# A two-layer decoder trunk on one core: joint 16 x 16 inverses for four heads, an SBUF region of its own for the first loads, and more of the modulation on VectorE

## The chip, the core and the metric

The kernel runs on one core of a Trainium2 chip. The metric is the device time of one execution in microseconds (us). "PE" is TensorE (its weight loads are listed apart as PEld), DVE is VectorE, ACT is ScalarE, POOL is GpSimd, SP is SyncE, which issues nearly all DMAs.

## The reference

The input x is [1, 256, 2048] and goes through two layers. In each layer six modulation rows m = 0 to 5 come from the condition c. They shift, scale and gate the two halves of a layer.

```python
c_act = jax.nn.silu(c)
for l in range(2):
    mod = c_act @ w_ada[l] + b_ada[l]              # [2048] x [2048, 6*2048]
    sh_m, sc_m, gt_m, sh_f, sc_f, gt_f = split(mod, 6)
    h = rms_norm(x, ln_mix[l]) * (1 + sc_m) + sh_m
    proj = h @ w_in[l]
    # 8 delta-net heads of 128 (q, k, v, gate z, beta, decay)
    # and 16 attention heads of 64 (2 kv heads, window 128, sinks, rope)
    mix = concat(gated_deltanet(...), attention(...)) @ w_out[l]
    x = x + gt_m * mix
    h = rms_norm(x, ln_ffn[l]) * (1 + sc_f) + sh_f
    gate, up = split(h @ w_gate_up[l], 2)          # 2 x 5632 columns
    x = x + gt_f * ((silu(gate) * up) @ w_down[l])
return rms_norm(x, ln_final)
```

A delta-net head works in chunks of 64 positions. Per chunk it needs the inverse of a unit lower triangular 64 x 64 matrix, then two products with it, then a recurrence over the four chunks:

```python
lower = where(strict, (k*beta) @ k.T * decay, 0) + eye
t_inv = triangular_solve(lower, eye)
w, u  = t_inv @ (k*beta*exp(g)), t_inv @ (v*beta)
```

## The kernel before

**Matrix products.** All weights are fp32 (603 MB are read). Each 128 x 1024 piece of weights is loaded by one DMA from the SP queue (line 115, called from `Weights.load`). A part of four 128 x 128 blocks is then split into a rounded copy `wh` (a cast on ACT) and a remainder `wl` (a subtraction on DVE, or on POOL when `Weights.split`, lines 336 to 365, finds GpSimd free outside the FFN). A block then costs three PE matmuls of 256 columns (tiles `pm`, in the head stages) or one of 512 and one of 256 (output projection and FFN). The activations sit in tiles `act`. All compute instructions pass through one helper, so that the profile gives them line 155; they are told apart by their tiles.

**Order.** Nothing is ordered by a scheduler at run time: the program counts a clock for each engine from prices (`Timed`, line 96) and emits each engine's instructions in the order in which this clock says they could go. Side work is written as generators in `Steps` (lines 217 to 285): each says which engine its next instructions go to, and is let forward 300 ns after its last one. Between two matmuls of a projection `S.tick()` lets them forward. `S.wait()` moves the clock by 100 ns where nothing can go. On the chip each engine then works strictly in that order.

**Stages.** (1) The first stage makes the modulations m = 1 and m = 0 of layer 0 and, while they become known k block by k block, partial projections of 28 tiles (`EARLY`, `GROUPS`). (2) The heads of layer 0. (3) The output projection of layer 0. (4) The FFN of layer 0. Then heads, output projection and FFN of layer 1. In the profile of before they lie at 0 to about 215, to 498, to 619, to 1381, to 1750, to 1845 and to 2604 us. These bounds are read from the first instruction that only the next stage has.

**Modulation** (`Ada`, line 457). A piece of w_ada is 128 x 1024 (tile `wada`, three buffers, 512 KB). Rows of layer 0 with m in `COLS` = (1, 0, 2, 4) are PE products (`products`, line 498): four matmuls 32 x 256 for each of 128 pieces, 8 records each in the trace. All others are DVE rows (`rows`, line 566): one multiply-and-sum instruction over 128 x 1024 for each piece (the profile calls it CUSTOM_DVE_ANT_0, the order below ISA), and after every second piece one 128 x 1 addition to `mod`. A table of due times says by which weight unit how many pieces must have been loaded. Before the first row, c's activation is spread over 128 partitions by four matmuls with `con` (line 534), after the last product.

**A delta-net head** (`delta`, line 1163). Scores k k^T and k q^T on PE; `B`, their product with decay and beta; `mc`, the sixteen 16 x 16 diagonal blocks gathered to 128 x 32 (lines 1227 to 1238). They are inverted for each head alone: `R` (line 1240), one fp32 matmul of 128 x 512 with it, then 30 chained multiply-and-sum instructions on DVE into `uc` (two for each of 15 columns, lines 1251 to 1259). `U` spreads `uc` to block diagonals (line 1264), PE transposes it together with v (`vT`, lines 1274 to 1277), and steps of 16, 32 and 64 rows make the whole inverse (tiles `W`, `y`, `yn`, lines 1289 to 1379). Then the recurrence, the norm and the gate follow.

Two heads may be in this part at once. `JOBS` (line 36) orders the projections: for each head k, q, an attention pair two ahead, v, z. Head h's v projection waits until head h - 2 has set "mid". This is set at line 1306, behind the copy of the first transposes and ahead of the steps of 16, 32 and 64.

## Time and profile before

| what | us |
|---|---|
| median of 3 runs | 2602.87 (2583.37 to 2609.12) |
| the profiled execution | 2606.06 |
| its span | 2604.2 |
| mean granted clock of TensorE | 0.983 |
| PE busy | 2500.6 (96%) |
| DVE busy | 1944.2 (75%) |
| ACT busy | 1281.5 (49%) |
| POOL busy | 417.9 (16%) |

The span is what the profiler shows from the first to the last instruction; 1.9 us of the execution lie around it. A share of busy time is an average over seven stages whose limits differ, so the table alone tells no stage's limit; the stretches in the prediction do.

### The profile page before, as it was taken

The numbers are of one execution on the slowest core, as the hardware profiler recorded it, in microseconds if no ns is written. First come the engines' busy times: TensorE is split into PE (matmuls) and PEld (weight loads), VectorE is DVE, ScalarE is ACT, GpSimd is POOL, SyncE is SP. The second block draws the span as 40 slices with busy tenths as digits, with TensorE's granted clock in tenths as the row PEclk, the third lists the DMA queues.
The fourth block names the chain that finished last, engine by engine and source line by source line (L and its number), as shares of the span: only waits on it lengthen the run. The fifth ranks groups of instructions, "written<-read, shape, count | busy, mean of one in ns | idle before, by whom it ended". The sixth has DMA issues, their size and how long they took to land.

```text
span 2604.2 us, 45895 instructions
## 1 busy us (share of the span) xinstructions
PE 2500.6 (96%) x16398; PEld 2148.0 (82%) x16398; DVE 1944.2 (75%) x4831; ACT 1281.5 (49%) x2759; POOL 417.9 (16%) x375
## 2 busy tenths in 40 slices
PE   6999999888999999999999899999899999999998
PEld 4777777777888888888888788998788888888887
DVE  3647777998777888888997877787877766555565
ACT  3225555335455444454445565644555544555553
POOL 2223333552000000000003443345000000000000
PEclk9999999999999999999999899999899999999999
DMA  8888664675777899999996433346577766555564
GB/s 279 294 286 290 241 211 171 222 253 187 259 253 252 311 323 323 324 328 330 324 346 204 163 123 121 130 162 203 194 265 249 261 187 188 196 190 188 184 195 137
DMA packets 184088, 608.62 MB, mean 234 GB/s; under 512 B 19121, under 2 KB 30513, under 8 KB 183857
## 3 DMA queue, kind: packets, MB, share of 16 engines
q1 hardware_dynamic: 183858, 605.68, 68.4%
q8 instruction: 128, 2.10, 0.3%
q14 instruction: 102, 0.84, 0.1%
HBM read 603.51 MB, written 2.10 MB: 233 GB/s over the span
## 4 chain that ended last, share of the span: by engine, by line
PE 42%; issue 30%; DVE 6%; ACT 1%; POOL 0%; POOLq 0%; DVEq 0%; ACTq 0%
PE pr L155 19%; PE psm L155 12%; PE pm L155 10%; DVE wl L155 1%; DVE wada L155 1%; DVE x L155 1%; ACT wh L155 0%; DVE act L155 0%; DVE R L155 0%; DVE mc L155 0%; DVE ry L155 0%; DVE sp_y L155 0%; DVE cv L155 0%; DVE do L155 0%; DVE B L155 0%
## 5 line engine op out<-in xcount | busy, mean ns | idle before, releaser
L155 ACT CAST wh<-w 128x512 fp32r<-128x512 f32 (+1 forms) x1566 | 900.9, 605 | 408.1 <-PE psm L155 137.7
L155 DVE TENSOR_TENSOR wl<-w,wh 128x512 fp32r<-128x512 f32 (+1 forms) x1317 | 893.3, 698 | 249.9 <-ACT wh L155 240.0
L155 PE MATMUL pr<-act,wh 128*128 128x512 f32 x2816 | 993.0, 397 | 10.8 <-DVE kq L155 7.5
L155 PE MATMUL pr<-act,wl 128*128 128x256 f32 x2816 | 792.8, 282 | 0.0
L155 PE MATMUL pm<-act,wh 128*128 128x256 f32 (+1 forms) x2816 | 658.6, 320 | 13.8 <-DVE x L155 5.0
L155 PEld LDWEIGHTS pr<-act,wh 128*128 128x128 f32 x2816 | 531.4, 189 | 137.5 <-DVE kq L155 8.1
L155 PE MATMUL psm<-act,wh 128*128 128x512 f32 (+1 forms) x1792 | 569.4, 373 | 1.8 <-ACT wh L155 0.9
L155 POOL TENSOR_TENSOR wl<-w,wh 128x512 fp32r<-128x512 f32 (+1 forms) x249 | 344.3, 1388 | 1272.0 <-ACT wh L155 1174.2
L155 PEld LDWEIGHTS pm<-act,wh 128*128 128x128 f32 x2816 | 462.7, 194 | 88.9 <-issue 44.6
L155 PEld LDWEIGHTS pr<-act,wl 128*128 128x128 f32 x2816 | 535.7, 190 | 0.0
L155 PE MATMUL pm<-act,wl 128*128 128x256 f32 x1664 | 474.3, 285 | 1.3 <-POOL wl L155 1.3
L155 PE MATMUL psm<-act,wl 128*128 128x256 f32 x1600 | 450.5, 282 | 1.7 <-POOL wl L155 1.7
L155 PEld LDWEIGHTS psm<-act,wh 128*128 128x128 f32 x1792 | 325.6, 190 | 72.5 <-issue 9.0
L155 DVE CUSTOM_DVE_ANT_0 wada<-wada,cs 128x1024 f32<-128x1024 f32 x256 | 325.5, 1274 | 36.6 <-DMA wada<-w_ada 36.2
L155 PEld LDWEIGHTS pm<-act,wl 128*128 128x128 f32 x1664 | 322.4, 194 | 2.2 <-POOL wl L155 1.7
L155 PEld LDWEIGHTS psm<-act,wl 128*128 128x128 f32 x1600 | 304.0, 190 | 2.7 <-POOL wl L155 2.1
L155 ACT COPY kq<-pr 128x512 f32<-128x512 f32 x88 | 51.8, 589 | 206.7 <-PE pr L155 206.6
L155 POOL TENSOR_TENSOR n2r<-ms,halfc 128x2 f32<-128x2 f32 x5 | 3.5, 691 | 797.9 <-DVE ms L155 797.9
L155 DVE TENSOR_TENSOR kq<-pr,kq 128x512 f32<-128x512 f32 x88 | 60.6, 688 | 92.8 <-ACT kq L155 92.8
L155 DVE SCALAR_TENSOR_TENSOR x<-psm,mod,x 128x256 f32<-128x256 f32 x128 | 61.9, 483 | 70.4 <-PE psm L155 67.9
L155 PE MATMUL psm<-wada,cs 128*32 128x256 f32 x1024 | 86.7, 414 | 17.7 <-DMA wada<-w_ada 17.5
L155 ACT CAST act<-kq 128x256 fp32r<-128x256 f32 x88 | 35.8, 407 | 74.0 <-DVE kq L155 74.0
(176 smaller groups left out, 1752.1 us busy)
## 6 DMA issues: line engine op xcount, KB each, us to landing
wada<-w_ada SPq DMA_DIRECT2D x384, 512.0 KB, 5.5
w<-w_gu SPq DMA_DIRECT2D x352, 512.0 KB, 4.6
w<-w_in SPq DMA_DIRECT2D x147, 512.0 KB, 4.0
w<-w_dn SPq DMA_DIRECT2D x128, 512.0 KB, 4.6
w<-w_out SPq DMA_DIRECT2D x64, 512.0 KB, 4.3
w<-w_dn SPq DMA_DIRECT2D x64, 384.0 KB, 4.2
w<-w_in SPq DMA_DIRECT2D x28, 384.0 KB, 4.9
x<-xT SPq DMA_DIRECT2D x4, 512.0 KB, 7.5
```

The lines of the kernel that those rows point to most:

```text
L155: return f(*a, **k)
```

## The change

**First stage.** `COLS` is (1,): only m = 1 of layer 0 is still made by PE products (32 pieces). Its 32 products alternate with the 32 pieces of m = 0, which are now DVE rows, and m = 2 and m = 4 (64 pieces) are DVE rows too. The first 64 pieces get eight buffers `wx` in a region laid out for this stage alone (before: three `wada`). Of the early weights every second piece gets one of four more buffers (`wy`) beside the four of `w`. c is spread (`spread`) at the start. Between the first stage and the heads stands a barrier: the head tiles are laid out when all of `hs`, the 64 first pieces and the first loads are done. FFN middles get eight tiles of their own (`mid`), and `act` goes from 38 to 30.

**Joint inverses.** `delta` is cut in three: `scores` per head up to `mc`, `inverses` per four heads, `delta` per head for the rest. `inverses` issues eight small DMAs on ACT's queue, which carry the `mc` of four heads to `qi` (64 partitions, one block in each, 256 elements). On DVE the block inverse is made in three doublings, 2 to 4 to 8 to 16, in `ui` (18 instructions, instead of four times 30). Eight DMAs bring it back to `uc`. R, its matmul and the subtraction ahead of it go. `JOBS` puts k and q of the next four heads ahead of the v of a batch. "mid" is now set behind the V transposes, which no longer stand with U's but behind the matmuls of the steps of 16, 32 and 64. The squares for q's norm move to `scores`; `y` exists twice (`y16`).

The order on the engines in the heads of layer 0, at the second batch (heads 4 to 7). On PE, before (`U` are the inverses of one head, `vT` its v, `con` the identity, `pm` a projection):

```order
L155 MATMUL pm_3078<-act_574,wh_2873 128x256 x2
L155 MATMUL pm_3078<-act_574,wl_2874 128x256
L155 MATMUL pm_3078<-act_630,wh_2873 128x256 x2
L155 MATMUL pm_3078<-act_630,wl_2874 128x256
L155 MATMUL psm_3103<-con_64,U_3047 128x128 x2
L155 MATMUL psm_3103<-con_64,vT_2557 128x128 x2
L155 MATMUL pm_3078<-act_955,wh_2916 128x256 x2
L155 MATMUL pm_3078<-act_955,wl_2917 128x256
L155 MATMUL psm_98<-wada_2985,cs_66 32x256 x4
```

and after, from the last projection matmuls ahead of the joint inverse (`w` and `av` are attention):

```order
L161 MATMUL pm_5176<-act_2091,wh_5105 128x256 x2
L161 MATMUL pm_5176<-act_2091,wl_5106 128x256
L161 MATMUL psm_5297<-con_67,w_1234_5090 128x128 x3
L161 MATMUL psm_5309<-w_1279_5291,av_2264 64x128
L161 MATMUL psm_5309<-w_1284_5307,av_2264 64x128
```

```order
L161 MATMUL psm_5415<-yn_5428,U_5372 32x32
L161 MATMUL psm_5445<-W_5381,B_3714 64x64 x2
L161 MATMUL psm_5451<-W_5383,B_3836 64x64 x2
L161 MATMUL psm_5445<-U_5369,yn_5412 64x64 x2
L161 MATMUL psm_5451<-U_5372,yn_5428 64x64 x2
L161 MATMUL psm_5460<-con_67,vT_4834 128x128 x2
L161 MATMUL pm_5465<-act_273,wh_5137 128x256 x2
L161 MATMUL pm_5465<-act_273,wl_5138 128x256
```

Before, the transposes of U and v stand between matmuls of a projection. After, the 41 rows from 1502 to 1543 hold no projection matmul; the stretch ends with the transposes of `vT`, behind which the v projection of head 6 begins. A stretch of that kind (65 rows, with 126 DVE instructions beside it) stands at the first batch of layer 0, and one of 41 rows at the second batch of layer 1. In before, none is longer than 16 rows.

On ACT, after, at the same batch (`x8` are eight DMA issues, `V` and `W` as above):

```order
L161 ACTIVATE w_1234_5090<-w_1234_5090,aden_5168 128x256
L161 DMA qi_5252<-mc_3727 8x16x16 x8
L161 CAST wh_5280<-w_5071 128x512
L161 COPY w_1279_5291<-psm_5274 128x384
L161 ACTIVATE th_5293<-pm_5176 128x256
L161 COPY w_1284_5307<-psm_5297 128x384
L161 CAST act_5321<-psm_5309 128x256
L161 ACTIVATE th_5323<-cv_5158 128x256
L161 DMA uc_5360<-ui_2104 128x1x16 x8
L161 COPY W_5381<-psm_5375 128x256
```

The two groups of DMA issues stand between casts, copies and the activations of attention. Whatever follows the second group on ACT waits with it for `ui`.

On DVE, before, at the inverse of one head, and after, at the joint one:

```order
L155 TENSOR_TENSOR mc_2840<-mc_2840,con_64 128x32
L155 TENSOR_TENSOR R_2843<-mc_2840,con_64 128x512
L155 TENSOR_TENSOR act_367<-pm_2743,act_367 128x256
L155 TENSOR_TENSOR wl_2874<-w_2642,wh_2873 128x512
L155 TENSOR_TENSOR act_2867<-psm_2848,act_2867 128x256
L155 TENSOR_TENSOR act_367<-pm_2822,act_367 128x256
```

```order
L161 ISA wada_5156,n_1282_5303<-wada_5156,cs_69 128x1024
L161 ISA n_1282_5303 128x1
L161 COPY ui_2104<-qi_5252 64x8
L161 SCALAR_TENSOR_TENSOR cv_5158<-pm_5057,par_66,cv_5158 128x253
L161 ISA wada_5278,n_1282_5303<-wada_5278,cs_69 128x1024
L161 ISA n_1282_5303 128x1
L161 COPY ui_2104<-qi_5252 64x4x2x2
L161 TENSOR_TENSOR hi_5325<-ui_2104 64x8
L161 TENSOR_TENSOR ui_2104<-ui_2104,hi_5325 64x4x2
```

Rows of the modulation (`wada`) now stand between the steps of the inverse. Counted over the whole order, the DVE rows (pieces) are 0, 10 and 23 in the first stage, the heads and the output projection of layer 0 before, and 36 (32 of them `wx`), 53 and 39 after; later stages keep theirs. Parts of weights split by POOL are 39, 57 and 39 in these stages before, 39, 50 and 29 after.

The diff, cut to its core:

```diff
-NACT = 38
+NACT, NMID = 30, 8
...
+AHEAD, BATCH = 2, 4
 JOBS = [("ak", 0), ("av", 0)] + [("aq", h) for h in range(AHEAD)]
+for _h in range(BATCH):
+    JOBS += [("k", _h), ("q", _h)] + [("aq", AHEAD + _h // 2)] * (_h % 2)
 for _h in range(H):
-    JOBS += [("k", _h), ("q", _h)] + [("aq", _h + AHEAD)] * (_h + AHEAD < H) + [("v", _h), ("z", _h)]
+    JOBS += [("v", _h), ("z", _h)]
+    for _n in range(BATCH, H):
+        if _n - BATCH == _h:
+            JOBS += [("k", _n), ("q", _n), ("aq", _n)]
...
-COLS = (1, 0, 2, 4)
-ROWS = [(0, m) for m in (2, 4, 3, 5) if m not in COLS] + [(1, m) for m in (1, 0, 2, 4, 3, 5)]
+COLS = (1,)
+ROWS = [(0, m) for m in (0, 2, 4, 3, 5)] + [(1, m) for m in (1, 0, 2, 4, 3, 5)]
...
+    def tag(self, u):
+        return "wy" if u < self.marks["mix0"] and u % 2 else "w"
+    def room(self):
+        u = self.loaded
+        return sum(self.tag(v) == self.tag(u) for v in self.tiles) < self.BUFS
...
-                self.todo = [(0, m, j, i) for j in range(8) for m in (1, 0) for i in range(4)]
-                self.todo += [(0, m, j, i) for m in COLS[2:] for j in range(8) for i in range(4)]
-                self.cols = len(self.todo)
-                self.todo += [(l, m, k, i) for l, m in ROWS for k in range(KT) for i in range(2)]
-                self.last = {it[:2]: n + 1 for n, it in enumerate(self.todo)}
+                self.todo = []
+                for j in range(8):
+                    for i in range(4):
+                        self.todo += [(True, 0, 1, j, i), (False, 0, 0, 2 * j + i // 2, i % 2)]
+                self.first = len(self.todo)
+                self.todo += [(False, l, m, k, i) for l, m in ROWS[1:] for k in range(KT) for i in range(2)]
+                self.last = {it[1:3]: n + 1 for n, it in enumerate(self.todo)}
+                self.order = [n for n, it in enumerate(self.todo) if not it[0]]
...
-                        (135, "out0"), (162, "ffn0"), (192, "down0"), (345, "mix1"), (345, "out1"), (352, "ffn1"), (384, "down1")
+                        (110, "out0"), (160, "ffn0"), (192, "down0"), (340, "mix1"), (345, "out1"), (352, "ffn1"), (384, "down1")
...
+            def room(self):
+                n = self.nload - self.ndone
+                return n < (b.total["wx"] if self.nload < self.first else self.BUFS)
...
-                while self.ready and self.nstart < self.nload and self.tiles[self.nstart][1] <= S.now():
-                    n = self.nstart
+                while self.ready and self.nstart < len(self.order):
+                    n = self.order[self.nstart]
+                    if n not in self.tiles or self.tiles[n][1] > S.now():
+                        return
                     if (hush and n >= self.force) or not b.free["n2"]:
                         return
                     behind = max(0, self.want(u) - n)
-                    slack = 100 + 150 * behind if n >= self.force else 2000
+                    slack = 3000 if n < self.first else 100 + 150 * behind if n >= self.force else 2000
...
-        def delta(l, h, st, outs):
+        def scores(l, h, st, bt):
...
+            if "mc" not in bt:
+                bt["mc"], bt["n"] = b.t("mc", [128, BATCH, 2, 16], bufs=1), 0
             nc.vector.tensor_reduce(
-                out=mc, in_=mo.rearrange("p a (m c) -> p a c m", c=16), op=ALU.add, axis=mybir.AxisListType.X
+                out=bt["mc"][:, h % BATCH, :, :], in_=mo.rearrange("p a (m c) -> p a c m", c=16), op=ALU.add,
+                axis=mybir.AxisListType.X,
             )
             b.give("do")
+            st.update(B=B, qn=qn, rk=rk)
+            bt["n"] += 1
+            if bt["n"] == BATCH:
+                S.add(inverses(bt, bt["ui"]), 0)
+        def inverses(bt, ui):
+            yield A_
+            qi = b.t("qi", [64, 272], bufs=1)
+            for x_ in range(2 * BATCH):
+                nc.scalar.dma_start(
+                    out=qi[x_ * 8 : x_ * 8 + 8, 0:256].rearrange("m (i j) -> m i j", j=16),
+                    in_=bt["mc"][:, x_ // 2, x_ % 2, :],
+                )
+            nc.end += 2500
+            yield D_
+            nc.vector.tensor_copy(out=ui[:, 1:256:34], in_=qi[:, 1:256:34])
+            def parts(of, n):
+                t = 8 // n
+                v = of.rearrange("p (t r) -> p t r", t=t)[:, :, 0 : 2 * n * 16].rearrange("p t (i c) -> p t i c", c=16)
+                return lambda i, j: v[:, :, i * n : i * n + n, j * n : j * n + n]
+            yield D_
+            u2, tmp = parts(ui, 2), b.t("hi", [64, 64], bufs=1)
+            v, to = tmp[:, 0:8].rearrange("p (t i) -> p t i", t=4), u2(0, 1)
+            nc.vector.tensor_copy(out=to, in_=parts(qi, 2)(0, 1))
             nc.vector.tensor_tensor(
-                out=mc, in0=mc, in1=C("id16").unsqueeze(1).to_broadcast([128, 2, 16]), op=ALU.subtract
+                out=v, in0=to[:, :, :, 0], in1=u2(1, 1)[:, :, 0:1, 1].to_broadcast([64, 4, 2]), op=ALU.mult
             )
-            R = b.t("R", [128, 32, 16], bufs=1)
+            nc.vector.tensor_tensor(out=to[:, :, :, 1], in0=to[:, :, :, 1], in1=v, op=ALU.add)
+            yield D_
             nc.vector.tensor_tensor(
-                out=R, in0=mc.rearrange("p a c -> p (a c)").unsqueeze(2).to_broadcast([128, 32, 16]),
-                in1=C("nid16").unsqueeze(1).to_broadcast([128, 32, 16]), op=ALU.mult,
+                out=v, in0=to[:, :, 1, :], in1=u2(0, 0)[:, :, 0:1, 1].to_broadcast([64, 4, 2]), op=ALU.mult
             )
-            yield from b.take("psm", P_)
-            q = b.bank()
-            nc.tensor.matmul(q, C("same"), R.rearrange("p c k -> p (c k)"), start=True, stop=True)
-            qk = q.rearrange("p (a c k) -> p a c k", a=2, c=16)
-            yield D_
-            uc = b.t("uc", [128, 2, 16], bufs=2)
-            nc.vector.tensor_copy(out=uc, in_=C("id16").unsqueeze(1).to_broadcast([128, 2, 16]))
-            for c in range(1, 16):
-                for blk in range(2):
-                    junk = b.t("jk", [128, 16], bufs=2)
-                    nc.vector.tensor_tensor_reduce(
-                        out=junk[:, 0 : c + 1], in0=uc[:, blk, 0 : c + 1], in1=qk[:, blk, c, 0 : c + 1], scale=1.0,
-                        scalar=0.0, op0=ALU.mult, op1=ALU.add, accum_out=uc[:, blk, c : c + 1],
-                    )
-                if c % 5 == 0 and c < 15:
+            nc.vector.tensor_tensor(out=to[:, :, 0, :], in0=to[:, :, 0, :], in1=v, op=ALU.add)
+            for n in (4, 8):
+                t = 8 // n
+                tmp = b.t("R", [128, 512], bufs=1)[0:64, 0 : t * n**3].rearrange("p (t i j k) -> p t i j k", t=t, i=n, j=n)
+                half = b.t("hi", [64, 64], bufs=1)[:, 0 : t * n * n].rearrange("p (t i j) -> p t i j", t=t, i=n)
+                qn_, un_ = parts(qi, n), parts(ui, n)
+                for out, lhs, rhs in ((half, qn_(0, 1), un_(1, 1)), (un_(0, 1), un_(0, 0), half)):
                     yield D_
-            b.give("psm")
+                    for x_ in range(t):
+                        nc.vector.tensor_tensor(
+                            out=tmp[:, x_], in0=lhs[:, x_].unsqueeze(2).to_broadcast([64, n, n, n]),
+                            in1=rhs[:, x_].rearrange("p k j -> p j k").unsqueeze(1).to_broadcast([64, n, n, n]), op=ALU.mult,
+                        )
+                        nc.vector.tensor_reduce(out=out[:, x_], in_=tmp[:, x_], op=ALU.add, axis=mybir.AxisListType.X)
+            yield A_
+            uc = b.t("uc", [128, BATCH, 2, 16], bufs=2)
+            for x_ in range(2 * BATCH):
+                nc.scalar.dma_start(
+                    out=uc[:, x_ // 2, x_ % 2, :],
+                    in_=ui[x_ * 8 : x_ * 8 + 8, 0:256].rearrange("m (i j) -> m i j", j=16),
+                )
+            nc.end += 2500
+            bt["uc"] = uc
+        def delta(l, h, st, bt, y16, outs):
+            while "uc" not in bt:
+                yield N_
+            yield from b.take("head", D_)
...
+            while "v" not in st:
+                yield N_
+            yield from b.take("psm", P_)
+            q = b.bank()
+            for tb in range(2):
+                nc.tensor.transpose(q[:, tb * 128 : tb * 128 + 128], st["v"][:, tb * 128 : tb * 128 + 128], ident)
+            st["mid"] = True
...
+        while None in hs or ada.ndone < ada.first or first:
+            S.wait()
+        b.lay(HEADS)
...
+            sts, bts = {}, [{"ui": ui} for _ in range(H // BATCH)]
...
+                elif kind == "v":
+                    S.add(delta(l, h, sts[h], bts[h // BATCH], y16s[h % 2], outs), 0)
+                    while h > 1 and "mid" not in sts[h - 2]:
+                        S.wait()
+                    vT = b.t("vT", [128, T], bufs=2)
+                    project("v", h, lambda q, h=h, vT=vT, st=sts[h]: conv_silu(l, vT, q, 16 + h, st, "v"))
```

More of the change, by code (lines that the diff above doesn't have):

```diff
@@ L1301, in delta @@
             b.give("psm")
-            yield from b.take("cv", A_)
-            sq = b.t("cv", [128, T])
-            nc.scalar.activation(out=sq, in_=kq[:, 1, :], func=AF.Square)
-            b.give("kq")
-            st["mid"] = True
             yield from b.take("psm", P_)
@@ L1316, in delta @@
                 )
-            for tb in range(2):
-                nc.tensor.matmul(q[:, 256 + tb : 257 + tb], sq[:, tb * 128 : tb * 128 + 128], one, start=True, stop=True)
-            b.give("cv")
             yield D_
@@ L1379, in delta @@
             b.give("psm")
+            while "v" not in st:
+                yield N_
+            yield from b.take("psm", P_)
+            q = b.bank()
+            for tb in range(2):
+                nc.tensor.transpose(q[:, tb * 128 : tb * 128 + 128], st["v"][:, tb * 128 : tb * 128 + 128], ident)
+            st["mid"] = True
+            yield A_
+            V = b.t("V", [128, 2, 128], bufs=2)
+            for tb in range(2):
+                nc.scalar.activation(
+                    out=V[:, tb, :], in_=q[:, tb * 128 : tb * 128 + 128], func=AF.Copy, scale=rk[:, tb : tb + 1]
+                )
+            b.give("psm")
             y = b.t("dy", [128, 2, 128], bufs=2)
```

239 lines of the change are left out of this document (128 added, 111 removed).

## The prediction

> **What bounds the kernel now.** I read the busy times of the page first, then the engines in the seven stages, then the groups of instructions that the change removes, then the waits and the chain that ended last where those stages are.
>
> ```profile
> PE 2500.6 (96%) x16398; PEld 2148.0 (82%) x16398; DVE 1944.2 (75%) x4831; ACT 1281.5 (49%) x2759; POOL 417.9 (16%) x375
> ```
>
> The stages, with the first cut at 190 us, where the last piece for a PE product of m = 0 has been asked for (columns: span; busy us and records of five engines; PE clock, DMA share, GB/s):
>
> ```profile
> core 0: us, PE busy (x) PEld busy (x) DVE busy (x) ACT busy (x) POOL busy (x), PEclk, DMA share, GB/s
> 0.00:190.00 190.00, 163.38 (x1336) 122.94 (x1336) 90.75 (x195) 61.14 (x124) 46.60 (x41) 0.97 0.84 286
> 190.00:215.00 25.00, 24.64 (x217) 16.97 (x216) 12.79 (x28) 11.60 (x27) 6.35 (x7) 1.00 0.93 332
> 215.00:498.00 283.00, 270.51 (x2337) 214.60 (x2336) 230.17 (x982) 155.54 (x439) 110.26 (x113) 0.98 0.66 223
> 498.00:619.00 121.00, 107.28 (x628) 88.72 (x628) 115.64 (x272) 47.77 (x110) 60.65 (x40) 0.96 0.70 236
> 619.00:1381.00 762.00, 752.48 (x4241) 652.23 (x4242) 637.61 (x1211) 370.46 (x710) 1.98 (x2) 0.99 0.86 299
> 1381.00:1750.00 369.00, 350.96 (x2858) 322.79 (x2858) 288.94 (x1116) 207.32 (x542) 144.71 (x138) 0.97 0.43 145
> ```
>
> The FFN, 762 us here and much the same in layer 1, is PE's (99% busy) and is not touched. The first stage has no full engine: PE 163 of 190, DVE 91; the queue moved 286 GB/s. In the heads PE is nearly full (271 of 283), DVE has 53 us free. In the output projection of layer 0 it is the other way round: DVE 115.6 of 121, PE 107.3. So the change, which takes work from PE and gives it to DVE, gives it in layer 0 to the engine that is full there. The chain that ended last shows that too: at 574 to 583 us it runs along DVE.
>
> ```profile
> 574.73 1.04 DVE wada L155
> 575.77 1.69 DVE wl L155
> ...
> 589.20 0.69 DVE wl L155
> ```
>
> The same remainder `wl` takes 1.69 us at 575.8 and 0.69 at 589.2. At the first POOL was making a `wl` of its own, at the second not.
>
> **The change, part by part.** What it moves is in these rows: the pieces of the modulation, `uc` and `R` in the stretches they lie in (first query PE, PEld, DVE; second DVE; third PE, PEld, DVE, ACT), and the means.
>
> ```profile
> 0.00:215.00 215.00, 48.96 (x552) 11.66 (x552) 0.00 (x0) 0.98 0.85 291
> 215.00:498.00 283.00, 37.71 (x472) 9.30 (x472) 15.54 (x10) 0.98 0.66 223
> 498.00:619.00 121.00, 0.00 (x0) 0.00 (x0) 31.45 (x23) 0.96 0.70 236
> 1300.00:1365.00 65.00, 0.00 (x0) 0.00 (x0) 23.66 (x20) 1.00 0.97 342
> ```
> ```profile
> 215.00:498.00 283.00, 30.69 (x441) 0.98 0.66 223
> 498.00:619.00 121.00, 4.69 (x63) 0.96 0.70 236
> 1381.00:1750.00 369.00, 34.63 (x482) 0.97 0.43 145
> ```
> ```profile
> 215.00:498.00 283.00, 7.36 (x14) 2.11 (x14) 4.98 (x7) 0.00 (x0) 0.98 0.66 223
> 1381.00:1750.00 369.00, 8.78 (x17) 2.38 (x16) 6.47 (x8) 0.00 (x0) 0.97 0.43 145
> ```
> ```profile
> L155 DVE TENSOR_TENSOR wl<-w,wh 128x512 fp32r<-128x512 f32 x1239 | 860.7, 714 | 229.9 <-ACT wh L155 220.2 <-issue 4.8
> L155 DVE SCALAR_TENSOR_TENSOR mod<-n,mod 128x1 f32<-128x1 f32 x128 | 31.4, 247 | 0.0
> L155 DVE TENSOR_TENSOR R<-mc,con 128x512 f32<-128x512 f32 x16 | 12.1, 759 | 0.5
> L155 DVE TENSOR_REDUCE mc<-do 128x32 f32<-128x256 f32 x16 | 9.6, 601 | 0.6
> ```
> ```profile
> PE psm L155 <- DMA wada<-w_ada: 17.5, 5, 14.3
> ```
>
> *First stage, 0 to 215.* PE loses 37 of 69 products (552 records by 8): 49.0 x 37/69 = 26 us, and gains the spreading of c, 5 us or less. DVE gains 32 rows, at 31.45/23 = 1.37 us, and 16 additions of 0.25: 48 us on 104, so 152, which still fits beside the stage. What sets the end is the arrival of the pieces: PE waited 17.5 us for `wada` in 5 waits. The queue moved 286 x 190 = 54.3 MB by 190 us; the same bytes at the 332 GB/s of the next stretch take 164. With some 4 us for a start and the last rows, the own region with eight buffers can give at most 22 us, and at least nothing if the rate stays. More buffers let the queue run past a late product, so I take near the upper end: **-18**. The barrier and the last DVE row ahead of the last `act` (1.4 + 0.25 us and three steps) are in that.
>
> *Heads and output projection of layer 0, 215 to 619, 404 us.* PE loses 37.7 (products) and 7.4 (R): 378 becomes 333. DVE has 230.2 + 115.6 = 345.8. From it go 30.7 + 4.7 (`uc`) and 5.0 (R), -40. Two joint inverses come: 4 instructions over 512 elements each, between 0.6 and 1.2 us (rows of R and mc), and 14 small ones at 0.25: 7.2 each, +14. By the order 92 rows stand here instead of 33: 59 x 1.37 = 81, and 30 additions, 7: +88. POOL splits 79 parts instead of 96, so DVE 17 more at 0.71: +12. Sum 420 us, more than the 404 there are. So DVE becomes the bound of both stages.
>
> How full it can be, the trace shows from both sides: 96% in the output projection (420/0.96 = 437, +33), and full, with rows at the 23.66/20 = 1.18 us that they take where POOL rests (409, +5). Into the time also go new waits, which lie in the stretches without a projection matmul. The first holds some 126 DVE instructions, at 230.17/982 = 0.23 us about 30 us in which PE has only small work. The second holds a chain: eight issues, landing, inverse 7 us, eight issues, landing, U, the steps. DVE has rows to do meanwhile, PE hasn't. A trip of such a DMA isn't in the trace. The nearest is the first small load on SP, 64 bytes a partition:
>
> ```profile
> 0.79 0.39 SPq L115 DMA_DIRECT2D cc<-c_col  x1
> ...
> 2.41 0.22 ACT L155 ACTIVATE th<-cc 128x16 f32<-128x16 f32 x1 [0.34 <-DMA cc<-c_col]
> ```
>
> 1.6 us from issue to use, and 8 issues of 0.4: some 5 us a trip. On ACT casts and copies stand behind the second group, which waits for `ui`; five parts of weights split ahead cover them, or it shows as PE waiting for `wh`. I take 430: **+26**, bounds +5 and +45 (the chain of 30 us half uncovered on top of 420).
>
> Rows beside POOL: in the output projection, with POOL busy 50%, a row takes 1.37 us, and 1.18 where POOL rests, 0.19 more; my sum holds 59 x 0.19 = 11 us for that. The Trainium skill (SBUF — State Buffer, "SBUF: two separate sides") says that DVE with two SBUF inputs and a GpSimd operation that reads SBUF take a shared pair of ports as an exclusive lock, so that the loser fully blocks. The trace agrees in direction, 1.69 against 0.69 us for `wl`; for the rows its mean gives a fifth of what a full block would. What that would make of the time is rival B.
>
> *Heads of layer 1, 369 us.* PE is the bound (351) and loses R: -8.8. DVE loses 41 and gains 14, which is worth nothing here. One stretch of 41 rows without a projection stands ahead of the v of head 6. It is the way from U to the transposes of `vT`: a hop from PE to DVE and back is
>
> ```profile
> 1769.03 0.29 DVE L155 TENSOR_SCALAR yn<-psm 64x128 f32<-64x128 f32 x1 [1.49 <-PE psm L155]
> ...
> 1770.66 0.28 DVE L155 COPY U<-psm 64x128 f32<-64x128 f32 x1 [1.34 <-PE psm L155]
> ```
>
> 1.63 us; seven of them and U are some 14 us, of which 7 are PE's own work. So +7, +4 for the way of `uc` behind a late inverse, and +2 for the clock: where PE had idled before 1430 us, 0.90 was granted.
>
> ```profile
> 1381.00:1430.00 49.00, 44.90 (x335) 40.28 (x335) 40.01 (x66) 29.20 (x65) 22.38 (x17) 0.90 0.54 177
> ```
>
> Together **+4**, bounds -9 (stretch filled) and +25 (twice as long, nothing saved). In the output projection of layer 1 DVE gets 6 parts fewer, **-2**. FFN: the 384 rows are as many as before there, 0.
>
> Sum: -18 + 26 + 4 - 2 = +10, from 2606 in the profiled execution: 2616. The median is 3 us lower, 2613; I take 2615.
>
> **Rivals.** *F, DVE stays covered.* Rows at 1.18 us, no new waits, the stretches filled by other work: -22 + 5 - 9 - 2 = -28, 2578. For it: POOL is used less, so DVE's price falls. Against it: DVE at 100% over 404 us, which no stretch shows. *S, small transfers come late (slower).* The 16 small DMAs of a batch share the engines with loads of 512 KB that are under way. If one waits for the loads ahead of it (four of `w`: 2 MB at 223 GB/s, 9 us), a trip takes 13 us instead of 5. Three batches have both trips on the path, the second inverse of each layer and the first of layer 0: 6 x 8 = +48, 2664. It decides from about 9 us a trip, where DVE's rows no longer fill the wait. For it: DMA share 0.66 in these heads. Against it: the first small load landed in 1.6 us, though in an empty queue. The Trainium skill (DMA: Bandwidth & Descriptors, "Queues, rings and completion order") has each DMA engine take turns between the queues with work, packet by packet, which speaks against S; no row before the change shows two queues at work. *B, moved rows wait out POOL's parts.* A row that meets one waits 1.4 us (a POOL part lasts about twice DVE's 0.71), and POOL is busy 42% of the 404 us (110.3 + 60.7): 59 x 0.42 x 1.4 = 35 in place of 11, +24, 2640. Against it: the 23 rows at 1.37 that stood there before. *N, the first stage doesn't do what it says.* Its rate stays at 286 GB/s, the rows only replace products: 0 for -18, so +28, 2634.
>
> **How the numbers follow.** Forecast 0.41, with its own range 2590 to 2640; F 0.24; S 0.15; N 0.15; B 0.05. About 1%, 26 us, is what a measurement of this kernel can tell from no change (its three runs lie 26 apart): faster is below 2577, slower above 2629. Faster: a little over half of F (0.14) and the forecast's lower tail, where both the first stage and the cover come out at their best (0.14): 0.28. Slower: S, B, about half of N and the forecast's upper tail (DVE as in the output projection): 0.15 + 0.05 + 0.08 + 0.08 = 0.36. Same: 0.36. The range reaches from 2566, below F's value by its tolerance of half the start's gain, to 2666, S's value; that leaves 0.1 out on either side.
>
> **What would show it.** In the profile after: no wait of PE on pieces of the first stage and over 310 GB/s to the heads' start, which then lies at about 197 (step 1). DVE over 95% busy from there to the FFN, PE below 80%, that stretch at 425 to 435 us (step 2). `qi` used some 5 us after the issue of its first DMA (13 by S). In layer 1 one gap of PE of 7 to 14 us ahead of the v of head 6, and a clock below 1 behind it (step 3). The prediction is wrong if the heads of layer 0 come out shorter than before with DVE below 90%, if the start is not earlier, or if the FFN moves.

## The result, and the profile after

The changed kernel takes 2671.9 us (median of 4 runs, 2668.9 to 2673.8), the kernel before 2606.0 beside it (4 runs): a ratio of 1.0277, 95% interval 1.0233 to 1.0320. It is slower by 2.8%, above the range of 2566 to 2666. The profiled execution has a span of 2667.2 us, 63 more than before, and a mean clock of 0.954 instead of 0.983.

To compare stages I cut both traces at the same first instructions (the first product of the betas, the first addition to x, the first `pr` product, and so on). The first stage, the heads and the output projection of layer 0 and the heads of layer 1, before:

```profile
0.00:208.30 208.30, 181.31 (x1489) 136.98 (x1489) 101.97 (x219) 67.92 (x139) 52.21 (x46) 0.98 0.86 293
208.30:498.20 289.90, 277.21 (x2398) 217.54 (x2397) 231.94 (x987) 160.56 (x451) 111.00 (x114) 0.98 0.66 224
498.20:624.30 126.10, 109.47 (x637) 90.09 (x637) 117.46 (x278) 50.11 (x113) 61.34 (x41) 0.95 0.67 226
...
1385.20:1749.50 364.30, 348.86 (x2850) 321.53 (x2851) 286.79 (x1108) 205.90 (x539) 143.52 (x136) 0.97 0.43 144
```

and after, all stages (columns as in the prediction: span; PE, PEld, DVE, ACT, POOL; clock, DMA share, GB/s):

```profile
0.00:194.10 194.10, 161.15 (x1189) 130.27 (x1190) 153.31 (x300) 68.05 (x140) 63.32 (x50) 0.96 0.88 313
194.10:534.80 340.70, 264.40 (x1994) 233.21 (x1994) 278.49 (x733) 162.27 (x459) 109.68 (x105) 0.82 0.49 164
534.80:670.50 135.70, 95.70 (x523) 80.40 (x521) 126.32 (x224) 45.93 (x98) 52.56 (x32) 0.88 0.80 275
670.50:1426.70 756.20, 747.06 (x4235) 649.57 (x4235) 637.70 (x1213) 369.71 (x709) 3.37 (x3) 0.99 0.87 303
1426.70:1809.10 382.40, 351.86 (x2886) 327.83 (x2887) 274.52 (x681) 206.93 (x544) 139.32 (x133) 0.94 0.40 137
1809.10:1905.40 96.30, 89.39 (x509) 77.25 (x507) 68.27 (x127) 46.02 (x90) 57.41 (x42) 0.97 0.62 216
1905.40:2667.20 761.80, 746.87 (x4234) 651.57 (x4234) 490.34 (x867) 382.04 (x717) 0.69 (x1) 0.99 0.61 201
```

The first stage is 14 us shorter. The heads of layer 0 are 51 us longer and the output projection 10: 416.0 has become 476.4. The heads of layer 1 are 18 us longer, the output projection there 6 shorter, and the FFNs 5 shorter and 9 longer. The heads and the output projection of layer 0 together are called the long stretch from here on. In it neither engine is full: DVE is busy 404.8 of 476.4 (85%), PE 360.1 (76%), at a clock of 0.82 and 0.88.

What PE waited for from 194 to 671 us (total, times, longest):

```profile
PE psm L161 <- DVE U L161: 25.4, 6, 15.3
PE psm L161 <- DVE do L161: 16.9, 1, 16.9
PE psm L161 <- DVE mod L161: 10.4, 1, 10.4
```

Before, the longest such waits from 208 to 625 us were on `U` too, but shorter:

```profile
PE psm L155 <- DVE U L155: 8.0, 2, 7.2
```

After, the 15.3 us stand ahead of the transposes of U in the second batch. The timelines of PE, DVE and ACT there:

```profile
461.37 2.20 PE L161 MATMUL psm<-w,av 128*64 128x128 f32 x12 [5.85 <-ACT w L161]
478.86 1.06 PE L161 MATMUL psm<-con,U 128*128 128x128 f32 x2 [15.30 <-DVE U L161]
```
```profile
463.41 0.17 DVE L161 COPY ui<-qi 64x8 f32<-64x8 f32 x1
...
475.68 0.68 DVE L161 TENSOR_REDUCE ui<-R 64x64 f32<-64x512 f32 x1
476.28 0.20 DVE L161 SCALAR_TENSOR_TENSOR mod<-n,mod 128x1 f32<-128x1 f32 x1
478.42 0.29 DVE L161 TENSOR_TENSOR U<-uc,con 128x128 f32<-128x128 f32 x1 [1.94 <-DMA uc<-ui]
479.10 0.29 DVE L161 TENSOR_TENSOR U<-uc,con 128x128 f32<-128x128 f32 x1 [0.39 <-DMA uc<-ui]
```
```profile
453.77 0.70 ACTq L161 DMA_DIRECT2D qi<-mc  x1
...
454.51 5.76 ACTq L161 DMA_DIRECT2D qi<-mc  x7
460.32 0.62 ACT L161 CAST wh<-w 128x512 fp32r<-128x512 f32 x1 [5.79 <-DMA qi<-mc]
...
476.39 5.59 ACTq L161 DMA_DIRECT2D uc<-ui  x8
482.03 0.65 ACT L161 COPY W<-psm 128x256 f32<-128x256 f32 x2 [17.56 <-DMA uc<-ui]
```

The joint inverse takes from 463.4 to 476.4 us on DVE, since five rows of the modulation (1.2 us each) and other work stand between its steps. ACT issues for 6.5 us at the first group (453.8 to 460.3, with an activation between) and for 5.6 at the second, where it also waits for `ui`; over all eight groups of the run it is 5.2 to 7.2 us, some 0.7 an issue. The first `uc` is used 2.0 us after its issue, each next one 0.7 us later. `qi`, of which DVE needs all eight parts, is used 9.6 us after the first issue (463.4 - 453.8): the issues take 6.5, and the last part lands 3.1 after them. From the first issue of `qi` to the first use of `uc` the way takes 24.6 us. The stretches around PE's two long gaps in the heads have these clocks:

```profile
310.00:350.00 40.00, 20.86 (x82) 15.65 (x81) 30.63 (x94) 13.74 (x39) 3.42 (x5) 0.54 0.22 66
...
455.00:480.00 25.00, 3.63 (x19) 2.06 (x17) 19.16 (x50) 2.44 (x6) 1.27 (x1) 0.60 0.41 130
```

The 16.9 and 10.4 us stand ahead of the FFN. There the queue loads pieces of the modulation alone, one every 1.8 us, and DVE makes their rows one by one:

```profile
627.66 8.31 SPq L121 DMA_DIRECT2D w<-w_gu  x4
639.28 27.02 SPq L121 DMA_DIRECT2D wada<-w_ada  x15
```

In the order 12 rows stand behind the last addition to x of this stage; before, none did.

### The profile page after: what moved, and what is told of

It is laid out like the page before. It is cut to its first block, busy times and chain, and to the rows that moved or that the text cites. A ratio compares the mean times of both kernels' runs of the same rounds, so it can differ in the third digit from the quotient of the medians.

```text
span 2667.2 us, 43580 instructions
## 1 busy us (share of the span) xinstructions
PE 2456.4 (92%) x15558; PEld 2150.1 (81%) x15558; DVE 2029.0 (76%) x4136; ACT 1281.0 (48%) x2754; POOL 426.3 (16%) x366
## 5 line engine op out<-in xcount | busy, mean ns | idle before, releaser
L161 ACT CAST wh<-w 128x512 fp32r<-128x512 f32 x1532 | 880.8, 604 | 437.3 <-PE pr L161 142.4
L161 PEld LDWEIGHTS pm<-act,wh 128*128 128x128 f32 x2816 | 473.5, 199 | 90.5 <-issue 33.6
L161 POOL TENSOR_TENSOR wl<-w,wh 128x512 fp32r<-128x512 f32 (+1 forms) x216 | 312.4, 1454 | 1262.0 <-ACT wh L161 1186.6
L161 DVE CUSTOM_DVE_ANT_0 wada<-wada,cs 128x1024 f32<-128x1024 f32 x320 | 406.8, 1274 | 44.1 <-DMA wada<-w_ada 43.8
L161 PE MATMUL psm<-act,wh 128*128 128x512 f32 (+1 forms) x1280 | 394.2, 366 | 1.1 <-DVE act L161 1.0
L161 PE MATMUL psm<-act,wl 128*128 128x256 f32 x1088 | 307.5, 283 | 0.4 <-DVE wl L161 0.3
L161 PEld LDWEIGHTS psm<-act,wh 128*128 128x128 f32 x1280 | 229.5, 190 | 48.5 <-issue 5.4
L161 PEld LDWEIGHTS psm<-act,wl 128*128 128x128 f32 x1088 | 207.0, 190 | 1.6 <-DVE wl L161 0.7
L161 PE MATMUL psm<-mid,wh 128*128 128x512 f32 x512 | 182.0, 393 | 0.0
L161 PE MATMUL psm<-mid,wl 128*128 128x256 f32 x512 | 144.8, 283 | 0.0
```

The costliest lines, as they stand in the source:

```text
L161: return f(*a, **k)
```

## The experiments

Three theories were weighed at first. R: the new rows on DVE make the loss. J: the way of the joint inverse (issues on ACT, landing, inverse, issues, landing, U) makes it. G: the late "mid" holds the v projections back. A fourth, Q, came with the rows ahead of the FFN. Medians are of 4 to 12 runs, each beside runs of the kernel before (medians 2597 to 2602); a ratio is to those. The times of stages are those of each run's one profiled execution.

**1. Short rows in the same order**

```diff
-out=w, in0=w, in1=ci            # rows, m = 2 and 4 of layer 0
+out=w[:, :64], in0=w[:, :64], in1=ci[:, :64]   # planned as 1024
```

> The changed kernel, but the 64 DVE rows of m = 2 and m = 4 of layer 0 multiply and sum 64 of each 1024 elements (so these two modulations are left incomplete). The order on every engine is that of the changed kernel. Theory R (DVE's new rows fill the heads and the output projection of layer 0): the 64 instructions shrink from 1.27 to about 0.15 us, some 70 us of DVE work go, and the stretch from the first stage to the FFN comes back from 476 to about 420 us, 2615 us in all. Theory J (PE stands in the way that the joint inverse takes: issues on ACT, landing, inverse, issues, landing, U): of the second batch's way only the 8 rows between the steps of the inverse go, 9 us, with some more elsewhere: 2645 to 2655.

2643.4 us, ratio 1.0175 (1.0124 to 1.0225). Some 27 us are gained, 24 of them in the long stretch (452.8). That is next to J's number, not R's. But the order still holds the wait ahead of the FFN, in which the pieces' loads set the pace, and everything else stands where it was planned for full rows: DVE is busy 64 us less and idles 112 us instead of 72. So with the order kept a us taken from DVE gives less than half a us; what it gives in an order made for it, the later pairs of runs show.

**2. One inverse for each head again**

```diff
-scores, inverses (4 heads), delta; JOBS with k, q ahead
+delta and JOBS of before
```

> The changed kernel with the inverse of each head alone again (R, its matmul, 30 chained instructions, the order of the projections of before, mid where it was); first stage, its region and the rows on DVE as changed. Theory R: DVE has 26 us more to do than in the changed kernel, so the heads of layer 0 stay long: 2640 to 2690. Theory J, and theory G (the late mid holds the v projection back): the 14 us of the first stage are kept and the stalls go; about 2600 to 2615, and no gap of PE over 6 us in the heads of either layer.

2654.4 us, ratio 1.0219 (1.0163 to 1.0276). R's number: without any joint inverse the loss is still 2.2%.

```profile
195.30:510.90 315.60, 257.63 (x1889) 222.03 (x1889) 279.50 (x1071) 155.42 (x437) 124.83 (x119) 0.89 0.53 174
510.90:670.00 159.10, 118.22 (x643) 96.91 (x643) 142.11 (x325) 52.87 (x121) 67.90 (x45) 0.85 0.71 239
```

The long stretch is 474.7 us, as in the changed kernel (476.4), with DVE at 89%. The heads of layer 1 are back at 366.9. So the new rows lengthen layer 0 this much without any joint inverse; with them in place the joint inverse takes 17 us of work from DVE and gains nothing there, and its own loss shows in layer 1.

**3. Copies in place of the small DMAs**

```diff
-for x_ in range(8): nc.scalar.dma_start(out=qi[...], in_=mc[...])
+for x_ in range(2): nc.scalar.copy(out=qi[:, 128 * x_ : ...], in_=mc[64 * x_ : ...])
```

(and the same for `uc`.)

> The changed kernel with each group of eight small DMAs replaced by two ACT copies of 64 x 128 (the blocks are not regrouped, so the inverses are of other numbers); the order on every engine is the same. Theory J: ACT is free of 8 x 5.5 us of issuing and the two landings of some 2 us go from each batch's way, so the gaps of 9 and 15 us ahead of U's transposes shrink by 8 to 10 us each and ACT's casts come earlier: 2672 becomes 2625 to 2640. Theory R: 2660 to 2670.

2648.3 us, ratio 1.0194 (1.0143 to 1.0245): 22 to 24 us, half of them in the heads of layer 1 (370.3). That lies between the two theories: J has a share, in both layers.

**4. The gate two heads later becomes three**

```diff
-while h > 1 and "mid" not in sts[h - 2]:
+while h > 2 and "mid" not in sts[h - 3]:
```

> The changed kernel, but the v of head h waits for the mid of head h - 3 (three vT buffers; the unused products go into B and dy for room). By the order the longest stretches of PE without a projection go from 65, 42 and 41 rows to 10, 35 and 12. Theory G: PE's gaps at the first batch of layer 0 and in layer 1 are filled, and the clock stays up: 2672 becomes 2625 to 2640. Theory J alone: ACT's issues hold back what the added projections need, the waits only move: 2660 to 2672. Theory R: no change, 2665 to 2672.

2667.2 us, ratio 1.0273 (1.0211 to 1.0335): 1 to 5 us, by the ratio or the median. The heads of layer 1 gain 10, layer 0 nothing. With DVE as it is, G alone is worth little.

**5. The due times of before**

```diff
-(110, "out0"), (160, "ffn0"), (192, "down0"), (340, "mix1")
+(135, "out0"), (162, "ffn0"), (192, "down0"), (345, "mix1")
```

> The changed kernel with the due times of before (135 pieces by the output projection, 162 by the FFN, instead of 110 and 160), so that 74 pieces instead of 53 stand in the heads of layer 0, 18 instead of 27 in the output projection, and none instead of 12 behind its last addition to x. Theory Q (the last pieces ahead of the FFN come too late: 28 us in which PE waits): the gaps of 10.4 and 16.9 us ahead of the FFN go, the heads get longer by less, 2645 to 2660. Theory R (DVE is what fills both stages): what the end gains the heads lose, 2665 to 2680.

2681.6 us, ratio 1.0322 (1.0266 to 1.0378). Q falls: the output projection shrinks from 135.7 to 105.2 us and the heads grow from 340.7 to 373.3. The long stretch is 478.5 us instead of 476.4: wherever the rows stand, they cost about the same.

**6 and 7. Neither rows nor joint inverse; joint inverse without rows.** Both have the short rows, this time also planned as short, and the due times of before.

> The changed kernel with the inverse of each head alone, the rows of m = 2 and 4 of layer 0 over 64 of 1024 elements (these modulations are left incomplete) and counted as so short in the order, and the due times of before. What is left of the change is the first stage with its region and the barrier, and 64 PE products less. If the rows and the joint inverse make the whole loss: the first stage keeps its 14 us, and PE's 38 us less give 10 to 25 us more in the heads: 2565 to 2590. If the barrier or the layout by stages costs something of its own: above 2600.

> The changed kernel with its joint inverse as it is, the rows of m = 2 and 4 of layer 0 over 64 of 1024 elements and counted so in the order (these modulations left incomplete), and the due times of before. It differs from the run with three costs taken away (2569 us) by the small DMAs and the gate alone, and from the run without joint inverses under the same rows (2584) by the joint inverse alone. Theory J (the way through the small DMAs and the late mid costs some 25 to 30 us in itself): 2595 to 2610, heads of layer 1 at 380. Theory R (rows make the loss, the joint inverse is free without them): 2570 to 2585.

With one inverse for each head 2584.2 us, ratio 0.9948 (0.9906 to 0.9990); with the joint one 2621.7, 1.0087 (1.0052 to 1.0121). The first:

```profile
193.40:473.30 279.90, 243.56 (x1884) 211.12 (x1883) 241.38 (x1136) 154.63 (x437) 98.31 (x105) 0.93 0.71 236
473.30:598.20 124.90, 109.29 (x646) 90.92 (x646) 114.66 (x279) 51.23 (x121) 61.85 (x41) 0.95 0.66 224
```

Against run 2, DVE has 421.6 - 356.0 = 66 us less to do in the long stretch and the stretch is 474.7 - 404.8 = 70 us shorter (the due times differ too; by run 5 they move the stretch by 2 us). And the joint inverse, as the change has it, costs 1.4% (some 36 us) where no rows hide it, more than J had foreseen: J holds too. By the traces some 32 us of it lie in the heads and output projections, half in each layer.

**8 and 9. The joint inverse with its suspected costs away, without and with rows.** Copies in place of the small DMAs, the gate of three, the due times of before.

> The changed kernel with joint inverses, but three of its suspected costs taken away at once: rows of m = 2 and 4 over 64 of 1024 elements and counted so, copies in place of the small DMAs, v waiting for the mid of h - 3, and the due times of before. If these are the joint inverse's costs, it beats one inverse for each head under the same rows (the run above) by R's matmul and DVE's 26 us: 2560 to 2590. If waits of the chain itself remain (theory J): 2600 to 2620.

> The run with three costs taken away (2569 us), but with the rows of m = 2 and 4 over all 1024 elements again: copies instead of small DMAs, v waiting for the mid of h - 3, due times of before. If a row costs what it takes on DVE whatever stands beside it (theory R): 89 us of DVE work come back and the heads and the output projection go from 392 to 455 to 470 us, 2630 to 2650. If the rows only hurt where they stand between the steps of the joint inverse's chain and nothing covers it: below 2610.

Without rows 2568.6 us, ratio 0.9888 (0.9834 to 0.9943), the lowest median of all, and the long stretch 391.7. With rows 2637.5, 1.0151 (1.0112 to 1.0190). By the ratios the rows cost 2.6% here, 68 us, and 61 between runs 7 and 5, 70 between runs 6 and 2: R, with nearly the same price beside three forms of the inverse. In the traces the long stretch grows by 57 us for 65 more on DVE (run 7 to 5), by 63 for 76 (run 8 to 9) and by 70 for 66 (run 6 to 2). Since the order was made anew for each, this is the price of a row together with the order that it brings. The small DMAs and the gate together are worth 52 us (run 7 to this), though in the changed kernel the gate alone gained at most 5 and the copies 24.

**10. The rows in halves.** Run 9 with each row of m = 2 and 4 as two instructions of 512 elements.

> The run with full rows and a clean joint inverse (2638 us), each row of m = 2 and 4 of layer 0 as two instructions over 512 elements (0.65 us in place of 1.22), in the same order. If DVE's sum decides: no gain, 2637 to 2650 (64 starts and 32 additions more, some 10 us of DVE). If the length of the block between steps of the chains decides: the scheduler's order is the same and both halves stand together, so a step waits as long; only a step that falls between the two halves could gain, and none does. So a gain of over 5 us would speak against both.

2646.6 us, ratio 1.0171 (1.0122 to 1.0219), 9 us more. In the trace DVE is busy 18 us longer in the long stretch, and the stretch is 15 us longer. No gain, as expected of the sum; the two halves stand together, so it does not exclude the block's length.

**11. PE products for m = 2 and 4 again, one inverse for each head.** Only the first stage is left of the change.

```diff
-COLS = (1,)
+COLS = (1, 2, 4)                # m = 0 stays with DVE
```

> The changed kernel with the inverse of each head alone and with m = 2 and m = 4 of layer 0 as PE products again (the due times of before); m = 0 stays on DVE, in the first stage. If the first stage's gain is real and free: 2583 to 2595, the heads and output projection of layer 0 at 410 to 420 us as before. If it is given back there: 2600 to 2610.

2590.9 us, ratio 0.9965 (0.9931 to 0.9998). The heads and the output projection of layer 0:

```profile
191.80:478.70 286.90, 276.44 (x2423) 219.58 (x2423) 228.89 (x990) 160.53 (x453) 108.09 (x115) 0.99 0.68 229
478.70:603.90 125.20, 105.43 (x605) 87.74 (x604) 110.90 (x266) 47.06 (x106) 59.99 (x38) 0.92 0.67 222
```

Run 6, in which PE is spared these products, took 404.8 us for the two instead of 412.1. This doesn't price PE alone: PE is busy 29 us less there, but DVE 16 us more, for the short rows and their additions. If these 16 us cost what DVE's cost elsewhere, PE's 29 are worth some 20 to 25 us; if they cost nothing, 7. No run takes work from PE alone.

**12 to 14. Whole kernels with joint inverses and PE products**, five `B` for room. With the gate of two, with the gate of three, and this with the small DMAs on SP's queue:

```diff
-nc.scalar.dma_start(out=qi[...] / uc[...], ...)
+nc.sync.dma_start(out=qi[...] / uc[...], ...)
```

> The same whole kernel with the gate as in the changed kernel (v of h waits for the mid of h - 2). Theory G: 10 to 20 us slower than with h - 3, half of it in the heads of layer 1. If the gate does nothing once the rows are gone: within 5 us of it.

> A whole kernel: first stage and joint inverses as changed, but m = 2 and 4 of layer 0 as PE products (due times of before), v waiting for the mid of h - 3, five tiles B for room. Theory R: with the rows gone the joint inverse's 26 us of DVE are of use where DVE is full, and the stretch from the first stage to the FFN falls below the 412 us of the same kernel with one inverse for each head: 2570 to 2585. Theory J: the small DMAs take it back, 2590 to 2605.

> The whole kernel with joint inverses, PE products for m = 2 and 4 and the gate of h - 3 (2599 us), its small DMAs issued on SP's queue instead of ACT's. If ACT standing 5.5 us at each group of issues is the cost: heads of layer 0 from 302 to about 290, of layer 1 from 378 to about 366, 2572 to 2582 us in all. If the way of the data is: no gain, 2595 to 2605; if loads behind them on SP come late: above 2605.

2614.7 (ratio 1.0066, 1.0042 to 1.0090), 2598.6 (1.0017, 0.9991 to 1.0043) and 2583.1 us (0.9945, 0.9913 to 0.9977). By the medians the gate and the move to SP are worth some 16 us each. The gate's gain is half in the long stretch and half in the heads of layer 1. The last kernel beats the changed one, and the kernel before by 0.5%; against run 11 its gain is within the intervals. Moving the issues shortens the heads of layer 0 from 302.2 to 284.5 us, of which the output projection gives 7 back (103.4 to 110.2):

```profile
190.80:475.30 284.50, 273.99 (x2451) 220.59 (x2451) 219.13 (x622) 160.56 (x453) 103.46 (x109) 0.99 0.70 236
475.30:585.50 110.20, 98.79 (x562) 82.59 (x560) 100.09 (x174) 48.08 (x107) 68.55 (x40) 0.95 0.71 248
...
1340.40:1718.90 378.50, 352.57 (x2861) 326.47 (x2862) 268.76 (x674) 203.85 (x532) 143.12 (x135) 0.94 0.43 139
```

The heads of layer 1, from which 12 us had been expected, stay at 378.5, where run 8 had 363.7. Whether the way of the data or the fifth instead of the sixth `B` keeps them there was not tried.

**15. As many constants as before.** Run 13 with 144 columns of zeros among the constants.

> The whole kernel with joint inverses, PE products and the gate of h - 3 (2599 us), with 144 columns of zeros among the constants, as many as the change took out, so that what lies behind them in SBUF lies as far as before. If the place of the tiles sets the FFN's rate: FFNs from 757 and 762 to about 751 and 753, 2580 to 2595 in all, and single runs spread by 1% as before's do. If not: 2595 to 2602.

2596.6 us, ratio 0.9991 (0.9963 to 1.0019); the FFNs 756.4 and 761.9. So the number of constants is not what lengthens them.

## Why the prediction was wrong, by its steps

The sum was +10 us; the profiled executions lie 63 apart. Of the 53 us between, 34 are in the long stretch, 14 in the heads of layer 1, 4 in the first stage and 5 in the FFNs; the output projection of layer 1 gives 4 back (-5.9 for -2).

**First stage: right.** -14.2 us for -18. It ends at 194.1 us (208.3 before; the 197 of the prediction belong to another mark, at 215) at 313 GB/s, and PE waits 6.0 us for pieces instead of 17.5.

**Heads and output projection of layer 0: the work was sized right, the share of DVE was not.** The sum of 420 us for DVE came out at 404.8, with 93 rows at 120.0/93 = 1.29 us. The step that failed is "how full it can be, the trace shows from both sides: 96% ... and full". It was 85%, so +60 us instead of +26, beyond the bound of +45. (That bound was added up wrongly as well: half of 30 us on top of 420 gives 435, +31.) I took the 96% from the output projection alone and left out the heads, since I had called them PE's ("In the heads PE is nearly full (271 of 283)"). By the same marks DVE had 349.4 of 416.0 there, 84%, and 420/0.84 = 500 would have been the sum, now too much. The runs show instead that each us more on DVE cost 0.8 to 1.1 us in the long stretch (the three pairs of runs), long before DVE was full: its idle time there took up little of the new work. It was 67 us before and 72 after, and between the runs of a pair it fell by 13 us at most. That the engines hand work to each other in a fixed order fits this, but was not shown to be the reason. What PE's work is worth in these heads was not isolated (run 11). PE's busy time also stretches as its clock falls: 45 us of products and R were taken from it and its busy time fell by 386.7 - 360.1 = 27.

**The end of the output projection: left out.** The 27 us ahead of the FFN could have been read in the order, where 12 rows stand behind the last addition. The loss is not in that place, though: run 5 moved the rows, the wait of 27 us went, and the long stretch was 2 us longer (the median 10, the rest in later stages).

**The joint inverse: the sign was wrong.** I credited it with 26 us of DVE and took its issues on ACT as covered ("five parts of weights split ahead cover them"). Run 7 shows some 36 us of cost. What failed is that cover: ACT stands 5.2 to 7.2 us at each of eight groups, and the v projections that could fill PE meanwhile wait for a "mid" behind the same chain. The way itself was priced too short: 5 + 7 + 5 us from the first issue to the use of `uc`, where 24.6 were measured, because a group of issues alone takes over 5 us and rows stand between the steps of the inverse (13 us instead of 7). Runs 12 to 14 give 16 us for the gate and as much for ACT's issues. With the small DMAs replaced and the gate moved (run 8) the joint inverse gains about 16 us, ratio 0.9888 against 0.9948; the intervals overlap, and its copies don't carry the blocks where they belong, so a whole kernel with this gain was not shown.

**Heads of layer 1: the place was right, the terms were not.** +18 us instead of +4. A gap ahead of the v of head 6 came, 7.7 us, within the 7 to 14 named. That is in part luck: it stands ahead of U's transposes, where `uc` comes late (+4 in the sum), while in the hops behind it (+7 in the sum) PE waits only some 2 us. Copies took back 12 of it, the gate 10, both all of it. The clock, for which I had put 2 us, took more: 0.94 over 382 us, where before had 0.97 over 364. PE's busy time rose by 3 us although R's matmuls, 8.8 us, had gone.

**FFN: put at 0.** The two moved by -4.7 and +9.3 us, which the prediction had named as a sign against it. The cause is open (see the last section).

**The rivals.** S gave a time near the measured one for a wrong reason. `qi` was indeed used later than the forecast's 5 us: 9.6 to 10.6 us after the first issue, past the 9 from which S was to decide. But most of that is ACT's issuing, 5.6 to 7.2 us, and not loads ahead in the DMA engines: in the second batch, where loads were under way, the last part landed 3.1 us after the last issue had ended. In the changed kernel's layer 0 the DMA engines were nearly idle when `uc` was under way (share 0.05 over the 2.0 us), so this trip alone can't test S. With loads from SP under way the first `uc` took 2.04 us from issue to first use in run 7 and 3.59 in run 13 (one line for each of the three trips; the last three columns are PE's clock, DMA share and GB/s):

```profile
476.39:478.42 2.03, 0.00 (x0) 0.00 (x0) 0.09 (x1) 0.00 (x0) 0.00 (x0) 0.50 0.05 4
444.29:446.33 2.04, 0.00 (x0) 0.00 (x0) 1.11 (x3) 0.00 (x0) 0.00 (x0) 0.50 0.53 173
300.43:304.02 3.59, 3.26 (x29) 2.51 (x28) 1.14 (x7) 0.00 (x0) 0.00 (x0) 1.00 0.92 283
```

So in these trips other loads cost up to some 1.6 us, not S's 8. That agrees with the turns between queues that the Trainium skill (DMA: Bandwidth & Descriptors, "Queues, rings and completion order") describes. B falls: a row took 1.29 us, less than the 1.37 before. F falls with the cover. N falls with the first stage.

**The clock.** The granted clock was 0.54 in the 40 us with a gap of 9.1 us and 0.60 around the one of 15.3. The Trainium skill (TensorE: Matmul & The Clock Gate, "What's actually happening") states half rate after an idle window of some 3.4 us, and full rate after as much sustained work. The trace agrees in kind: inside the gap of 15.3 us, from 476.4 to 478.4, 0.50 was granted. In the first of these stretches PE was busy 20.9 of 40 us. How much of the 60 us is clock and how much waiting was not separated.

## What to carry to other kernels

Where engines hand work to each other in a fixed order, don't expect an engine's idle time to take up new work, and don't take the fullest share seen in another stage for what the engine can reach. Here each us of rows added to a DVE that was 81 to 88% busy cost 0.8 to 1.1 us, with the order planned for it; with the order kept, shorter rows gave back less than half a us each. Work that is batched to save instructions can make a longer way, and whatever waits for its end (a gate for a buffer, the issuing engine) must be moved with it. Count what the issuing engine stands at a group of small DMAs, and consider a queue that nothing waits for: here that gained 16 us, none of it in the heads of layer 1.

## What was not expected of the hardware

A small DMA of 8 x 16 x 16 elements took 0.66 to 0.7 us to issue in a group of eight without a pause, on ACT as on SP (here SP, in run 14), where the first load of 128 x 16 took 0.39:

```profile
1492.13 5.27 SPq L1348 DMA_DIRECT2D uc<-ui  x8
```

So moving it to SP saved nothing of the issue itself, only ACT's time. The Trainium skill (DMA: Bandwidth & Descriptors, "Issuing engines are not separate DMA queues") says that DMAs started from several engines run on the same DMA engines, and that this saves only the time of starting them, usually small beside the DMA. Here a group of eight took 5.2 us or more on ACT, more than the 2.0 us from an issue to its use, and moving the groups gained 16 us in all by run 14.

The FFN of layer 1 took between 752.5 us (before) and 768.5 (run 11) in the profiled executions, at a clock of 0.99 in each and with no edit in it. In the kernels with joint inverses both FFNs lay at 755 to 766. Its cause is open; run 15 excludes only the length of the constants.
